# SwiGLU over 8192 rows: the one-row first tile moved to the end

## The chip, the cores and the metric

The kernel runs on one core of one Trainium2 chip, with the other cores idle. The metric is the device time of one execution in microseconds. One execution of the kernel was also recorded by the hardware profiler; its page names lines of the kernel (L54 is line 54) and these engines and queues: ACT (the scalar engine, here silu), DVE (the vector engine, here the product), POOL (GpSimd) and SP (the sync engine). All data between device memory (HBM) and on-chip memory (SBUF, 128 partitions) goes through the core's 16 DMA engines. A transfer is issued by SP, ACT or POOL; q1 is SP's queue, q10 is ACT's and q0 is POOL's.

## The reference

```python
# x: (8192, 8192) float32
def reference(x):
    a, b = np.split(x, 2, axis=-1)
    silu_b = b / (1 + np.exp(-b))
    return a * silu_b
```

Each row of x holds 4096 values of `a` and then 4096 of `b`; the result has 4096 values per row. 268.4 MB are read and 134.2 MB written, and there is nothing to reuse.

## The kernel before, in words

The 8192 rows are cut into 33 tiles. `rows[i]` (line 23) says how many consecutive rows each of the 128 partitions gets of tile i: one for the first, two for the next 31, one for the last. A two-row tile takes 256 rows of x: a load of 8.39 MB (64 KB in a piece per partition) and a store of 4.19 MB (32 KB in a piece per partition). A one-row tile is half of that on both sides.

There are three slots in SBUF, each as large as a two-row tile, and tile i uses slot i % 3. In a slot silu overwrites `b` (line 54), the product goes to the front of the same slot (line 56), and the store reads it from there (line 63). So a slot is free for tile i + 3 only when the store of tile i has landed: the load on line 45 waits for `stored[i - 3]`. These are the only waits that matter. `behind` leaves out all others that the tile framework would add, and the order of instructions is the written one (`manual_schedule`).

Before the loop, the loads of tiles 0, 1 and 2 are issued by SP (line 67). Then for each tile the loop does the compute (`swiglu`), issues the store and issues the load three tiles on. The stores of tiles 0 to 29 are issued by ACT, but those of tiles 17 and 19 by POOL. The stores of the last three tiles (30, 31 and 32) are issued by SP, whose program order is: load 31, load 32 (which waits for store 29), store 30, store 31, store 32. Each waits in turn, so none of them passes the one ahead.

The compute of a tile is one ACTIVATE and one TENSOR_TENSOR over the whole tile, with two exceptions, where both are cut into two pairs: tile 0 (one row) by column halves, and the second to last tile (two rows) by rows.

Of the kernel before, what the change touches and what calls it, by code (L numbers as in the profile page):

```python
# [1 line left out]

# [4 lines left out]

_SILU = mybir.ActivationFunctionType.Silu


@with_exitstack
def kernel(
    ctx: ExitStack,
    tc: tile.TileContext,
    x: bass.AP,
    out: bass.AP,
):
    nc = tc.nc
    N, M = x.shape  # L20
    half = M // 2
    P = nc.NUM_PARTITIONS
    rows = [1] + [2] * (N // (2 * P) - 1) + [1]
    first = [P * sum(rows[:i]) for i in range(len(rows))]
    last = len(rows) - 1

    pool = ctx.enter_context(tc.tile_pool(name="sbuf", bufs=1))
    ctx.enter_context(tc.manual_schedule())
    slots = [pool.tile([P, 2 * M], x.dtype, name=f"slot{s}") for s in range(3)]
    touched = [[] for _ in slots]  # L30
    newest = {}
    landed, made, stored = {}, {}, {}

    def behind(inst, s, *targets):
        for t in touched[s]:
            if t not in targets and t is not newest.get(inst.ins.engine):
                tc.declare_no_dep(inst.ins, t.ins, reason="ordered by the other waits")
        touched[s].append(inst)
        newest[inst.ins.engine] = inst
        return inst  # L40

    def load(i):
        s, r = i % 3, rows[i]
        src = x[first[i] : first[i] + P * r].rearrange("(p r) m -> p (r m)", r=r)
        inst = nc.sync.dma_start(out=slots[s][:, : r * M], in_=src)  # L45
        behind(inst, s, *([stored[i - 3]] if i >= 3 else []))
        landed[i] = inst

    def swiglu(i, k0, k1, c0, c1):
        s, r = i % 3, rows[i]  # L50
        v = slots[s][:, : r * M].rearrange("p (k s c) -> p k s c", k=r, s=2)
        to = slots[s][:, : r * half].rearrange("p (k c) -> p k c", k=r)
        b = v[:, k0:k1, 1, c0:c1]
        gate = nc.scalar.activation(out=b, in_=b, func=_SILU)  # L54
        behind(gate, s, landed[i])
        prod = nc.vector.tensor_mul(out=to[:, k0:k1, c0:c1], in0=v[:, k0:k1, 0, c0:c1], in1=b)  # L56
        behind(prod, s, gate, *([made[i]] if i in made else []))
        made[i] = prod

    def store(i, engine):  # L60
        s, r = i % 3, rows[i]
        dst = out[first[i] : first[i] + P * r].rearrange("(p r) m -> p (r m)", r=r)
        inst = engine.dma_start(out=dst, in_=slots[s][:, : r * half])  # L63
        behind(inst, s, made[i])
        stored[i] = inst

    for i in range(3):
        load(i)
    for i in range(last + 1):
        if i == 0:  # L70
            swiglu(i, 0, 1, 0, half // 2)
            swiglu(i, 0, 1, half // 2, half)
        elif i == last - 1:
            swiglu(i, 0, 1, 0, half)
            swiglu(i, 1, 2, 0, half)
        else:
            swiglu(i, 0, rows[i], 0, half)
        if i < last - 2:
            store(i, nc.gpsimd if i in (17, 19) else nc.scalar)
            load(i + 3)  # L80
        else:
            store(i, nc.sync)


# [1 line left out]
_INS = ['x']  # L86
_OUTS = [((8192, 4096), 'float32')]


# [23 lines left out]
```

## Time and profile before

| | |
|---|---|
| median of 3 runs | 935.07 us (934.93 to 935.09) |
| the profiled execution | 935.77 us, span 934.0 us |
| DVE busy | 278.5 us, 35 instructions |
| ACT busy | 226.6 us, 36 instructions (one is a table load of 1.3 us) |
| DMA | 402.67 MB, 431 GB/s over the span |
| two-row store on ACT's queue | 27 of them, 36.3 us from issue to landing (median) |
| two-row store on POOL's queue | 2 of them, 33.0 us |
| load on SP's queue | 34.9 us (median of 31) |
| one ACTIVATE of 128x8192, 128x4096, 128x2048 | 7.03, 3.61, 1.90 us |
| one TENSOR_TENSOR of 128x8192, 128x4096, 128x2048 | 8.69, 4.42, 2.29 us |

The span is what the profiler saw of the execution; the time around it belongs to the launch. "Busy" counts an engine's own instructions; the DMA row on the page gives the mean busy share of the 16 DMA engines in 40 equal slices of the span (9 is 90% or more). In a windows view, each line is a stretch of the span with its length, the busy times of DVE, ACT and POOL with instruction counts, the clock of the matrix engine (not used here), the DMA share and the GB/s. A packet is counted where it ends, so a short window can read above or below what was moving. In a timeline, each line has start, time, engine and line, operation, operand shapes and count, and in brackets how long the engine had been idle and what ended that; an issue that stands for several (x4) has the time from the first to the last. The chain view follows the work that ended last back from the end, each step with its start and its time.

### The profile page before, as it was taken

To read this page: it belongs to the slowest core of one execution; us is meant where nothing else is said; L and a number is where in the kernel's file an instruction comes from. 1 tells how busy PE (TensorE), PEld (TensorE's weight loads), DVE (VectorE), ACT (ScalarE), POOL (GpSimd) and SP (SyncE) were. 2 spreads that over 40 slices of the span, in tenths; PEclk is the share of its full clock that TensorE was granted. 3 is DMA by queue.
4 is the path that set the end of the run, shared out by engine and by line. 5 is a ranking of instruction groups with operands and counts; after the bars stand their busy time and mean duration, and the time that the engine had idled before them with its cause. 6 is when DMAs were issued, how large, how long until landed. Compare 5 with 4: busy or idle time off the path is not lost.

```text
span 934.0 us, 215 instructions
## 1 busy us (share of the span) xinstructions
DVE 278.5 (30%) x35; ACT 226.6 (24%) x36; POOL 1.4 (0%) x6
## 2 busy tenths in 40 slices
DVE  1131333123331233311333113332133321333242
ACT  2332023320333203332023320333202333023330
POOL 0000000000000000000000000000000000000000
DMA  9999999999999999999999999999999999999998
GB/s 404 404 466 410 427 449 427 448 422 453 406 455 420 428 446 449 425 418 457 408 445 431 425 439 436 448 427 429 446 406 449 428 427 448 428 425 462 435 406 383
DMA packets 9505, 402.67 MB, mean 431 GB/s; under 512 B 1056, under 2 KB 1056, under 8 KB 1056
## 3 DMA queue, kind: packets, MB, share of 16 engines
q1 hardware_dynamic: 5184, 278.92, 69.1%
q10 hardware_dynamic: 4032, 115.35, 28.6%
q0 software_dynamic: 288, 8.39, 2.1%
q14 instruction: 1, 0.01, 0.0%
HBM read 268.44 MB, written 134.22 MB: 431 GB/s over the span
## 4 chain that ended last, share of the span: by engine, by line
DMA 78%; DVE 11%; ACT 9%; another core or an unknown queue 1%; issue 0%; SPq 0%; ACTq 0%
DMA slot<-in_x_dram 40%; DMA out_dram<-slot 37%; DVE slot L56 11%; ACT slot L54 9%; SPq L45 0%; ACTq L63 0%
## 5 line engine op out<-in xcount | busy, mean ns | idle before, releaser
L56 DVE TENSOR_TENSOR slot<-slot 128x8192 f32<-128x8192 f32 (+2 forms) x35 | 278.5, 7960 | 638.5 <-ACT slot L54 638.4
L54 ACT ACTIVATE slot<-slot 128x8192 f32<-128x8192 f32 (+2 forms) x35 | 225.3, 6443 | 685.2 <-DMA slot<-in_x_dram 685.2
L63 POOL DMA_DIRECT2D out_dram<-slot x2 | 1.2, 598 | 569.8 <-DVE slot L56 569.8
L54 ACT ACT_TABLE_LOAD x1 | 1.3, 1283 | 0.7 <-PEq L97 0.7
L97 POOL MEMSET const-bfloat16-1.0<- 128x1 bf16 x1 | 0.1, 101 | 0.0
L97 POOL MEMSET const-float32-0.0<- 128x1 f32 x1 | 0.1, 98 | 0.2 <-issue 0.2
L97 POOL MEMSET const-float32-1.0<- 128x1 f32 x1 | 0.1, 98 | 0.0
L97 POOL MEMSET const-uint8-127<- 128x1 uint8 x1 | 0.1, 98 | 0.0
## 6 DMA issues: line engine op xcount, KB each, us to landing
out_dram<-slot ACTq DMA_DIRECT2D x27, 4096.0 KB, 36.3
slot<-in_x_dram SPq DMA_DIRECT2D x2, 4096.0 KB, 13.7
out_dram<-slot POOLq DMA_DIRECT2D x2, 4096.0 KB, 33.0
out_dram<-slot SPq DMA_DIRECT2D x2, 4096.0 KB, 20.5
out_dram<-slot ACTq DMA_DIRECT2D x1, 2048.0 KB, 28.1
out_dram<-slot SPq DMA_DIRECT2D x1, 2048.0 KB, 16.1
slot<-in_x_dram SPq DMA_DIRECT2D x31, 34.9
```

Of the source, the lines that this page charges most:

```text
L54: gate = nc.scalar.activation(out=b, in_=b, func=_SILU)
L56: prod = nc.vector.tensor_mul(out=to[:, k0:k1, c0:c1], in0=v[:, k0:k1, 0, c0:c1], in1=b)
L63: inst = engine.dma_start(out=dst, in_=slots[s][:, : r * half])
L97: nc = _bacc.Bacc("TRN2", target_bir_lowering=False, num_devices=1)
```

## The change

The list of rows per partition becomes 31 twos and then two ones. Tile 0 is now a two-row tile, cut by rows into two pairs of instructions, as the second to last tile was. The second to last tile is now a one-row tile and has one pair, as the last. The number of tiles, the number of loads and stores of each size, the slots, the three loads ahead and the engines that issue are unchanged; tiles 1 to 30 have the same sizes as before and begin 128 rows earlier in x, and the tile of each index keeps its slot and its issuing engine.

```diff
-    rows = [1] + [2] * (N // (2 * P) - 1) + [1]
+    rows = [2] * (N // (2 * P) - 1) + [1, 1]
     first = [P * sum(rows[:i]) for i in range(len(rows))]
     last = len(rows) - 1
...
     for i in range(last + 1):
         if i == 0:
-            swiglu(i, 0, 1, 0, half // 2)
-            swiglu(i, 0, 1, half // 2, half)
-        elif i == last - 1:
             swiglu(i, 0, 1, 0, half)
             swiglu(i, 1, 2, 0, half)
         else:
```

## The prediction

> **What bounds the kernel now.** I read the page's head and its queue table first, then windows over the whole run and over its ends, then the timeline, the chain and the DMA issues.
>
> ```profile
> span 934.0 us, 215 instructions
> DVE 278.5 (30%) x35; ACT 226.6 (24%) x36; POOL 1.4 (0%) x6
> DMA  9999999999999999999999999999999999999998
> ...
> q1 hardware_dynamic: 5184, 278.92, 69.1%
> q10 hardware_dynamic: 4032, 115.35, 28.6%
> q0 software_dynamic: 288, 8.39, 2.1%
> ```
>
> The two compute engines are busy under a third of the span. The three queues' packets took 69.1 + 28.6 + 2.1 = 99.8% of 16 engines' span, 932.1 of 934.0 us. So the 16 DMA engines are the bound, and only about 1.9 us of the span is not their packet time.
>
> ```profile
> 0.00:1.00 1.00, 0.00 (x0) 0.27 (x1) 0.20 (x4) 1.00 0.00 0
> ...
> 583.87:873.88 290.01, 86.92 (x10) 70.29 (x11) 0.00 (x0) 1.00 1.00 434
> ...
> 932.00:933.00 1.00, 0.00 (x0) 0.00 (x0) 0.00 (x0) 1.00 0.04 16
> 933.00:934.00 1.00, 0.00 (x0) 0.00 (x0) 0.00 (x0) 1.00 0.00 0
> ```
>
> The last two columns are DMA share and GB/s. The engines stand still in the first microsecond and in the last two, and work at a share of 1.00 and 434 GB/s in between. A two-row tile moves 8.39 MB in and 4.19 MB out; at 434 GB/s that is 19.3 + 9.7 = 29.0 us, which is the distance of the tiles in the timeline (583.87, 612.88, 641.88).
>
> ```profile
> 0.74 47.06 SPq L45 DMA_DIRECT2D slot<-in_x_dram  x4
> 12.88 3.71 ACT L54 ACTIVATE slot<-slot 128x2048 f32<-128x2048 f32 x2 [10.86 <-DMA slot<-in_x_dram]
> 14.82 4.49 DVE L56 TENSOR_TENSOR slot<-slot 128x2048 f32<-128x2048 f32 x2 [14.82 <-ACT slot L54]
> 19.35 0.38 ACTq L63 DMA_DIRECT2D out_dram<-slot  x1
> ...
> 864.66 29.33 SPq L45 DMA_DIRECT2D slot<-in_x_dram  x2
> 873.88 7.03 ACT L54 ACTIVATE slot<-slot 128x8192 f32<-128x8192 f32 x1 [21.97 <-DMA slot<-in_x_dram]
> 880.94 8.69 DVE L56 TENSOR_TENSOR slot<-slot 128x8192 f32<-128x8192 f32 x1 [20.31 <-ACT slot L54]
> 894.04 23.32 SPq L63 DMA_DIRECT2D out_dram<-slot  x3
> 899.22 7.12 ACT L54 ACTIVATE slot<-slot 128x4096 f32<-128x4096 f32 x2 [18.31 <-DMA slot<-in_x_dram]
> 902.87 8.96 DVE L56 TENSOR_TENSOR slot<-slot 128x4096 f32<-128x4096 f32 x2 [13.23 <-ACT slot L54]
> 908.93 3.62 ACT L54 ACTIVATE slot<-slot 128x4096 f32<-128x4096 f32 x1 [2.59 <-DMA slot<-in_x_dram]
> 912.58 4.42 DVE L56 TENSOR_TENSOR slot<-slot 128x4096 f32<-128x4096 f32 x1 [0.75 <-ACT slot L54]
> ```
>
> The idle times in brackets are compute waiting for loads. The last load is issued at 893.66 and lands by 908.9; the last product ends at 917.0, and stores alone run until 932.
>
> ```profile
> 860.67 32.98 DMA out_dram<-slot
> ...
> 893.66 15.24 DMA slot<-in_x_dram
> ...
> out_dram<-slot ACTq DMA_DIRECT2D x1, 2048.0 KB, 28.1
> ```
>
> The chain goes through the slots (store, then the load that waited for it). It names whose transfer was in the way; it is not a sum of delays, because the DMA engines are full meanwhile. The last line, the only one-row store on ACT's queue, serves below.
>
> **The DMA work.** Before: 31 two-row and two one-row loads, as many stores. After: the same counts and sizes. On q1 there are 36 transfers either way (33 loads, three stores), on q10 28 and on q0 two. 5184 packets over 36 transfers is 144 each, of which the page counts 16 as under 512 B (1056 over 66 transfers), so each of 128 partition lines is one packet: 64 KB for a two-row load, 32 KB for a two-row store or one-row load, 16 KB for a one-row store. At 434/16 = 27.1 GB/s per engine these take 2.42, 1.21 and 0.60 us, and an engine has 8 of each transfer. Packet work removed: 0; added: 0. q10 gains 2.1 MB that q1 loses. The change can therefore pay only by idle time, of which 1.9 us exists, and can cost only by opening new idle time.
>
> **Compute.** The two 128x2048 pairs of tile 0 go (ACT 3.7, DVE 4.5 us). The 30 whole pairs stay; of 128x4096 there are four pairs instead of three: two on the new tile 0 and one on each one-row tile. Before: 30 x 8.692 + 3 x 4.425 + 2 x 2.288 = 278.6 us on DVE; after: 30 x 8.692 + 4 x 4.425 = 278.5. One instruction less on each engine. All of it lies beside transfers: cost 0.
>
> **The start.** The first transfer needs about 2.4 us beyond its bytes: issued at 0.74, landed at 12.86, and 4.19 MB at 434 GB/s are 9.7. The first load of 8.39 MB then lands at 0.74 + 2.4 + 19.3 = 22.5. Its two halves take what the two halves of the two-row tile at 899.22 took until 911.83, 12.6 us, so the first store is issued at 35.1 instead of 19.35. All three first loads, 25.2 MB, are issued in the first microseconds and would keep the engines full alone until 0.74 + 2.4 + 58.0 = 61.1. The 15.8 us of later start are hidden by these loads with 26 us to spare; without that cover they would cost 15.8. Load 3 waits for store 0 at SP, with nothing ahead of its turn but loads. Taken: 0.
>
> **The middle.** A slot's round is 3 x 29.0 = 87 us: 15.75 of compute, a load and a store. At first store plus load landing are 36.3 + 34.9 us, after the two POOL stores 33.0 + 38.5 (806.69 to 844.86 is 38.2). Only their split moves. After the change, store 0 competes with two-row loads at 2.42 + 1.21 us a pair of packets: 29 us, landing near 35.1 + 1.0 + 29 + 1.4 = 66.5 (of the 2.4 us I put 1.0 before the bytes and 1.4 after). At 36.1 the loads still have some 10.3 MB, which at two thirds of 434 GB/s last until 71.8, so load 3, issued at 66.5, waits behind load 2 and lands at 71.8 + 29 + 1.4 = 102.2. Store 1 lands at 65.1 + 29 + 1.4 = 95.5 and issues load 4, so each queue always has its next transfer, with a few us to spare. At DMA share 1.00, a later load is an earlier store and costs nothing. ACT's queue is passed by one more two-row store instead of a one-row one; POOL's stores stay at indices 17 and 19, now 4.19 MB later in the rows. Taken: 0.
>
> **The tail.** Let T be the landing of load 30, now the last two-row one. Store 28 has landed at T - 9.2 (864.66 against 873.86), which issues load 31, one row; it starts when load 30's data end, about T - 1.4. Until then store 29 got one 32 KB packet per 64 KB packet; with some 9.5 us at 3.63 a pair, 2.6 of its 8 packets. The other 5.4 go one for one against load 31's 32 KB packets, 13.1 us, to T + 11.7. Load 31 then has 2.6 left, alone, 3.1 us, to T + 14.8. Load 32 needs 1.4 us for store 29's landing and 1.0 for its own first bytes: it arrives at T + 14.1. That cover of 0.7 us is thin. With the earlier split (34.9) the same steps give 1.6 packets, 2.0 us of cover against 2.4, a hole of 0.4 us. What lies under it is the full latency, 2.4 us, if load 31 is through before store 29. Nothing excludes small gains at transfer edges, at most some 0.5 us of the 1.9 idle. I take 0, since the split of the late rows is the nearest, and keep -0.5 and +2.4.
>
> Behind it the queue is full: store 30 is made at T + 15.75 and stands behind load 32 on q1, load 32's data end at T + 24.5, stores 30 and 31 last until T + 39, and store 32 is ready by T + 24.5 + 1.4 + 8.1 (908.93 to 917.0) + 1.0 = T + 35. SP now holds store 30 from 889.6, when it is made, until 894.04, behind load 32's wait; after the change load 32 is issued by T + 13.1 and store 30 is made later, so nothing is held.
>
> The row behind the split is the one-row store on ACT's queue: 8 x (2.42 + 0.60) + 2.4 = 26.6 us if packets alternate; equal bytes would give 12.1, two load bytes per store byte 16.9. Measured: 28.1. So packets alternate. In the Trainium skill, the page DMA: Bandwidth & Descriptors, section Queues, rings and completion order, says the same of each engine: it goes round its queues and takes a whole packet from one before it switches; by that rule load 31 and store 29 share evenly and the sum is 0, while two load bytes per store byte (what 8.39 and 4.19 MB in 29 us each look like) would end load 31 at T + 13.6 and store 29 at T + 15.3, and the hole would be the full 2.4. The trace agrees with the page in this row.
>
> **Sum:** 0 + 0 + 0 + 0 on the profiled execution's 935.77 us (934.0 of span and 1.77 around it), which stands 0.70 above the median of 935.07; so 935.8 profiled and 935.1 in the median.
>
> **The rivals.** *A hole in the tail* (slower): load 31 runs out before load 32 arrives. For it: 0.7 us of cover by the sum above, and SP's order, by which store 30 cannot step in. Against it: the alternation. Price 0.4 to 2.4 us, likeliest 1.9, 937.0; it decides when load 31's data end before store 29 lands.
>
> *An exposed start* (slower): the first store's 15.8 us delay reaches the end, 935.1 + 15.8 = 950.9. It would need the loads to be done before 35.1 us; they last until 61.1. The Trainium skill's page Perfetto Trace Analysis, section DMA Optimizations, says that splitting transfers can let work start sooner and finish sooner when DMA engines are generally idle; merging the small first load is the reverse. The trace does not meet its condition: 99.8% busy.
>
> *A gain*: four tile distances are longer than 29.0 us (30.25 and 30.21, 29.44 and 29.45), 3.4 us together, and another phase avoids them: 931.7. Against it: the windows over them move 434 to 441 GB/s, so what the loads lost the stores had.
>
> *Holes in every round* (slower): both queues empty at once for 0.1 us a tile, 31 x 0.1, 938.2. Against it: each has its next transfer waiting.
>
> **How the numbers follow.** No change 0.70 (935.1, own range 934.6 to 935.9); hole in the tail 0.20; exposed start 0.04; gain 0.03; holes in every round 0.03. About 0.2%, 1.87 us, is what a measurement of this kernel can tell from no change: below 933.2 is faster, above 936.9 slower. Half the tail-hole case lies above: slower 0.10 + 0.04 + 0.03 = 0.17, faster 0.03, same 0.80. The range goes from 934.5 to 937.5 (935.1 + 2.4) and leaves out 0.10.
>
> **What the profile after would show.** The first store issue near 35 us on ACT's queue and load 3 near 66; tile distances of 29.0; queue shares that again sum to 932 us; load 31 and load 32 landing 10 us apart, with no 1 us window near zero between; last product some 10 us before the end. I am wrong if a window near load 32's issue falls to nothing, if queue shares sum well below 99.8% of the span, or if the packets themselves take longer (the sum rises with the span).

## The result and the profile after

The changed kernel takes 938.09 us in the median of 22 runs (936.69 to 938.94) against 935.07 us for 22 runs of the kernel before (934.89 to 939.29): a ratio of 1.0027, 95% interval 1.0020 to 1.0033. The median is 3.0 us slower, just beyond the 0.2% that the prediction named as its bound, and 0.6 us above the top of its range. The profiled execution took 937.95 us, 2.18 us more than the one of before, which stood 0.70 above its median; its span is 936.2.

The head of the page after and its queue table (packets, MB, share of 16 engines' span):

```profile
span 936.2 us, 213 instructions
DVE 278.5 (30%) x34; ACT 226.5 (24%) x35; POOL 1.4 (0%) x6
...
q1 hardware_dynamic: 5184, 276.83, 68.6%
q10 hardware_dynamic: 4032, 117.44, 29.1%
q0 software_dynamic: 288, 8.39, 2.1%
```

The counts of packets are those of before, and the three shares again sum to 99.8%. But they are shares of a longer span: the times of all packets, summed and divided by 16 engines, are 933.9 us, against 931.9 before. The DMA engines are as full as ever by this table; the same packets took 1.9 us longer. In the tail some 32 KB packets took up to 2.46 us where 1.21 is the median, so lost time is counted there as packet time, and the table cannot show a hole of this size. What shows it is the distance between two landings. The timeline of the changed kernel, first its start and then its tail:

```profile
0.73 127.46 SPq L45 DMA_DIRECT2D slot<-in_x_dram  x6
22.63 7.12 ACT L54 ACTIVATE slot<-slot 128x4096 f32<-128x4096 f32 x2 [20.62 <-DMA slot<-in_x_dram]
...
35.27 0.38 ACTq L63 DMA_DIRECT2D out_dram<-slot  x1
46.59 7.03 ACT L54 ACTIVATE slot<-slot 128x8192 f32<-128x8192 f32 x1 [16.84 <-DMA slot<-in_x_dram]
```

```profile
888.82 7.03 ACT L54 ACTIVATE slot<-slot 128x8192 f32<-128x8192 f32 x1 [22.00 <-DMA slot<-in_x_dram]
895.88 8.69 DVE L56 TENSOR_TENSOR slot<-slot 128x8192 f32<-128x8192 f32 x1 [20.33 <-ACT slot L54]
901.32 0.33 SPq L45 DMA_DIRECT2D slot<-in_x_dram  x1
904.53 3.62 ACT L54 ACTIVATE slot<-slot 128x4096 f32<-128x4096 f32 x1 [8.68 <-DMA slot<-in_x_dram]
...
915.89 3.62 ACT L54 ACTIVATE slot<-slot 128x4096 f32<-128x4096 f32 x1 [7.75 <-DMA slot<-in_x_dram]
```

The chain shows what load 32 waited for, store 29:

```profile
875.58 25.73 DMA out_dram<-slot
901.30 0.02 issue
901.32 14.55 DMA slot<-in_x_dram
```

Load 32 is issued at 901.32, when store 29 has landed; load 31 has landed by 904.53 and load 32 by 915.89. The two landings are 11.36 us apart, where the 4.19 MB need 9.7; in the kernel before they were 9.71 apart (899.22 and 908.93). That is 1.65 us of DMA time lost between two loads. The windows between these landings, before and then after (the last two columns are DMA share and GB/s), say the same:

```profile
899.22:908.93 9.71, 5.96 (x2) 7.12 (x3) 0.00 (x0) 1.00 1.00 432
```

```profile
904.53:915.89 11.36, 4.47 (x2) 3.61 (x1) 0.00 (x0) 1.00 0.97 378
```

The rate falls from 432 to 378 GB/s while the share of busy time is still 0.97.

### The profile page after: what moved, and what is told of

Read it like the earlier page. It is cut to its first block, busy times and chain, and to the rows that moved or that the text cites. A ratio compares the mean times of both kernels' runs of the same rounds, so it can differ in the third digit from the quotient of the medians.

```text
span 936.2 us, 213 instructions
## 1 busy us (share of the span) xinstructions
DVE 278.5 (30%) x34; ACT 226.5 (24%) x35; POOL 1.4 (0%) x6
## 4 chain that ended last, share of the span: by engine, by line
DMA 78%; DVE 11%; ACT 9%; another core or an unknown queue 1%; issue 0%; SPq 0%; ACTq 0%
DMA slot<-in_x_dram 41%; DMA out_dram<-slot 36%; DVE slot L56 11%; ACT slot L54 9%; SPq L45 0%; ACTq L63 0%
## 5 line engine op out<-in xcount | busy, mean ns | idle before, releaser
L56 DVE TENSOR_TENSOR slot<-slot 128x8192 f32<-128x8192 f32 (+1 forms) x34 | 278.5, 8190 | 645.5 <-ACT slot L54 645.4
L54 ACT ACTIVATE slot<-slot 128x8192 f32<-128x8192 f32 (+1 forms) x34 | 225.2, 6627 | 692.3 <-DMA slot<-in_x_dram 692.3
```

## The experiments

The cover of a waiting load is the load data still queued when it is issued; where the cover is too short, a hole opens. Two theories stood against each other. *Tail*: load 32, which waits for store 29, comes when load 31 is nearly through, and the queues run dry. *Start*: something in the new first tile costs, although the DMA engines have loads queued until 61 us.

**The wait taken away.** Tile 32 uses the free second half of tile 31's slot, so that its load needs only store 28.

```diff
+    def place(i):
+        if i == last:
+            return (last - 1) % 3, rows[i], M
+        return i % 3, rows[i], 0
...
-        behind(inst, s, *([stored[i - 3]] if i >= 3 else []))
+        behind(inst, s, *([stored[min(i, last - 1) - 3]] if i >= 3 else []))
...
-            load(i + 3)
+            if i + 3 < last:
+                load(i + 3)
+            if i + 3 == last - 1:
+                load(last)
```

> The changed kernel, but the load of tile 32 goes to the unused second half of slot 1, beside tile 31, and is issued right behind load 31: it no longer waits for store 29. If the hole in the tail (load 32 arriving after load 31's data have run out, about 1.5 us by the distance of their landings, 11.4 us against 9.7 before) is the main cost, loads 31 and 32 land 9.7 us apart or less and the time falls by about 1.5 us, to 936.6. If the cost lies at the start, the time stays at 938.1.

Measured: 936.33 us (935.97 to 937.09), ratio to the kernel before 1.0011 (1.0002 to 1.0019). In its timeline the landings are 9.72 us apart:

```profile
850.26 29.79 SPq L50 DMA_DIRECT2D slot<-in_x_dram  x3
...
904.22 3.62 ACT L59 ACTIVATE slot<-slot 128x4096 f32<-128x4096 f32 x1 [8.66 <-DMA slot<-in_x_dram]
...
913.94 3.62 ACT L59 ACTIVATE slot<-slot 128x4096 f32<-128x4096 f32 x1 [6.11 <-DMA slot<-in_x_dram]
```

The last load has now been issued by 850.26 + 29.79 = 880.1, far ahead. The tail theory gave 936.6; 1.8 us are gone. But 1.2 us over the kernel before (935.15 in this group of runs) remain, and the tail does not hold them.

**The start undone.** Tile 0 is loaded and stored as two one-row parts, the first computed by column halves as before; `part`, `swiglu_part` and `store_part` load, compute and store one such part.

```diff
-    for i in range(3):
-        load(i)
...
+    part(0, 0)
+    part(0, 1)
+    load(1)
+    load(2)
...
-            swiglu(i, 0, 1, 0, half)
-            swiglu(i, 1, 2, 0, half)
+            swiglu_part(0, 0, 0, half // 2)
+            swiglu_part(0, 0, half // 2, half)
+            store_part(0, 0)
+            swiglu_part(0, 1, 0, half)
+            store_part(0, 1)
```

> The changed kernel, but tile 0 is loaded and stored in two one-row parts, the first computed by column halves, so the first store is one row and goes out near 19.4 us as in the kernel before. If the start costs about 0.5 us, the time falls to about 937.6; if only the tail costs, it stays at 938.1 (one load and one store more).

Measured: 937.28 us (935.20 to 938.54), ratio 1.0016 (1.0007 to 1.0026): 0.8 us less than the changed kernel. The profiled execution is the fastest of its eleven, 935.20 us, and in it the landings of loads 31 and 32 are 9.70 us apart, though load 32 still waits for store 29:

```profile
847.72 52.29 SPq L45 DMA_DIRECT2D slot<-in_x_dram  x3
...
903.32 3.62 ACT L55 ACTIVATE slot<-slot 128x4096 f32<-128x4096 f32 x1 [8.69 <-DMA slot<-in_x_dram]
...
913.02 3.62 ACT L55 ACTIVATE slot<-slot 128x4096 f32<-128x4096 f32 x1 [6.08 <-DMA slot<-in_x_dram]
```

This time there is no hole: half of the engines had landed load 31 3.3 us after load 32's issue, where it was 1.9 in the changed kernel's trace. The cover is thus not the same in every trace; more of it below.

**Both edits.**

> Both edits, the early load 32 and the split first tile. If hole and start together are the whole difference, 935.1 to 935.6, the time of the kernel before; if something else in between costs, it stays above 936.5.

Measured: 935.24 us (935.04 to 936.97), ratio 1.0002 (0.9991 to 1.0013), the median of the kernel before. Within the interval, about 1 us either way, tail and start together are the whole difference, and nothing in the tiles between them was seen to cost. The median needs care: the eleven times fall into two groups, six at 935.0 to 935.2 and five at 936.5 to 937.0. The profiled execution is of the second group (936.52); its landings at the end are in step (9.69 us apart), its packets take 932.1 us an engine, 0.2 more than in the kernel before, and its last landing comes 1.47 us after that of the fifteenth of the sixteen engines. That points to one engine behind the others, not to a hole.

**The tail alone.** The kernel before keeps its start, but its last rows are cut 2, 1, 1, 1; the last two tiles share a slot and are issued together, behind the wait for store 29.

```diff
-    rows = [1] + [2] * (N // (2 * P) - 1) + [1]
+    rows = [1] + [2] * (N // (2 * P) - 2) + [1, 1, 1]
...
```

> The kernel before with its start unchanged, but its last five rows per partition cut as 2, 1, 1, 1 (the last two share a slot and are issued together), so that load 31 is a one-row load and load 32 waits for store 29 as in the changed kernel. If the tail hole is the main cost, about 935.1 + 1.5 = 936.6; if the start is, 935.1.

Measured: 937.99 us (935.99 to 938.77), ratio 1.0023 (1.0014 to 1.0031): more than expected. Its three last landings:

```profile
889.12 3.62 ACT L59 ACTIVATE slot<-slot 128x4096 f32<-128x4096 f32 x1 [8.68 <-DMA slot<-in_x_dram]
...
899.50 3.62 ACT L59 ACTIVATE slot<-slot 128x4096 f32<-128x4096 f32 x1 [6.77 <-DMA slot<-in_x_dram]
...
911.03 3.62 ACT L59 ACTIVATE slot<-slot 128x4096 f32<-128x4096 f32 x1 [7.91 <-DMA slot<-in_x_dram]
```

They are 10.38 and 11.53 us apart, 2.5 us over two times 9.7. The second distance is odd, since those two loads were issued together. This version also has one tile more, which is a rival for its time.

**The same cut, but covered.** Loads 31 and 32 now share a slot and are issued together after store 28; the load that waits for store 29 is load 33, with both in front of it. The edit is against the version just shown.

```diff
     def place(i):
+        if i == last - 1:
+            return (last - 2) % 3, rows[i], M
         if i == last:
-            return (last - 1) % 3, rows[i], M
+            return (last - 1) % 3, rows[i], 0
...
-        behind(inst, s, *([stored[min(i, last - 1) - 3]] if i >= 3 else []))
+        behind(inst, s, *([stored[i - 3 - (i >= last - 1)]] if i >= 3 else []))
...
```

> The kernel with the old start and last rows 2, 1, 1, 1, but now the load that waits for store 29 is the last one, behind two one-row loads that were issued together, so 9.7 us more of load are queued when it is issued. If the thin cover of that wait made the 2.8 us of the version before this one, 935.1 to 935.4; if the extra tile or the one-row shapes did, it stays near 938.

Measured: 935.32 us (935.20 to 937.20), ratio 1.0002 (0.9993 to 1.0011), with the landings in step again:

```profile
888.75 3.62 ACT L61 ACTIVATE slot<-slot 128x4096 f32<-128x4096 f32 x1 [8.68 <-DMA slot<-in_x_dram]
...
898.48 3.62 ACT L61 ACTIVATE slot<-slot 128x4096 f32<-128x4096 f32 x1 [6.12 <-DMA slot<-in_x_dram]
...
908.19 3.62 ACT L61 ACTIVATE slot<-slot 128x4096 f32<-128x4096 f32 x1 [6.09 <-DMA slot<-in_x_dram]
```

The shapes, the counts and the wait on store 29 are those of the version before; what differs is which load waits, and so what stands in the queue ahead of it. So neither the extra tile nor one-row shapes cost anything that shows, and the difference between the two versions, 2.7 us by the medians and 2.0 by the ratios, is the thin cover.

**One load instead of two, and the changed kernel beside it.** The last two rows are loaded as one two-row tile (32 tiles of two rows), computed and stored by rows. In the same group of runs the changed kernel was timed once more.

```diff
-    rows = [2] * (N // (2 * P) - 1) + [1, 1]
+    rows = [2] * (N // (2 * P))
```

> The changed kernel, but the last two one-row tiles are loaded as one two-row tile (32 tiles, all of two rows), computed and stored by rows in two parts. No load waits behind a one-row load any more. If the thin cover makes the tail hole, 936.3 like the version with the early load 32; if two one-row stores and computations at the end cost, 938.1.

> The changed kernel itself, beside the others of this call: 938.1, if it differs from the version with one two-row load at the end only by the tail hole, 1.8 us above that version.

Measured: 936.11 us (935.38 to 936.28), ratio 1.0008 (0.9999 to 1.0017), and 937.72 us (937.62 to 938.95, five runs) for the changed kernel, ratio 1.0033 (1.0020 to 1.0045). In the second trace of the changed kernel the hole is there again, 11.30 us between the landings:

```profile
904.27 3.62 ACT L54 ACTIVATE slot<-slot 128x4096 f32<-128x4096 f32 x1 [8.66 <-DMA slot<-in_x_dram]
...
915.57 3.62 ACT L54 ACTIVATE slot<-slot 128x4096 f32<-128x4096 f32 x1 [7.68 <-DMA slot<-in_x_dram]
```

The hole is worth 1.6 us here, and avoiding it in this way gives about the same time as the early load 32 (936.33).

**What at the start costs.** Four versions with the early load 32 vary only the start. In one, tile 0 is computed whole, which delays the first store:

```diff
-        if i == 0:
-            swiglu(i, 0, 1, 0, half)
-            swiglu(i, 1, 2, 0, half)
-        else:
-            swiglu(i, 0, rows[i], 0, half)
+        swiglu(i, 0, rows[i], 0, half)
```

> The early load 32 (no tail hole), with tile 0 computed in one piece, so that the first store goes out 3.1 us later, at 38.4 us, after the load packets that begin at 36 to 38.5 us. If the start's 1.2 us come from the first store entering just at the boundary between loads 1 and 2 (load packets of 3.7 us instead of 2.4 near 38.7), another moment changes them: 935.2 to 935.8. If they come from the first store being two rows, or from loads of 64 KB packets alone, the time stays at 936.3.

Measured: 936.85 us (936.23 to 937.39), ratio 1.0018 (1.0009 to 1.0027). The first store went out at 38.55, and the time did not fall:

```profile
38.55 0.38 ACTq L68 DMA_DIRECT2D out_dram<-slot  x1
...
72.18 7.03 ACT L59 ACTIVATE slot<-slot 128x8192 f32<-128x8192 f32 x1 [23.06 <-DMA slot<-in_x_dram]
```

But the edit did more than move the store. Load 2 has landed by 72.18, and store 0, now later, lands only at 72.34; load 3 waits for it and is issued at 72.36 with no load ahead of it, a wait as in the tail with no cover at all. Packets that begin at 75.4 to 78.9 take 1.34 us an engine too long in this trace, while those near the first store's entry, at 41.1 to 41.7, take 0.96, against 1.18 with the early load 32 alone (how this is worked out stands below). So this run does not settle whether the moment of the first store matters. In two others only the stores or only the load of tile 0 are split into rows:

```diff
+            swiglu_part(0, 0, 0, half)
+            store_part(0, 0)
+            swiglu_part(0, 1, 0, half)
+            store_part(0, 1)
```

> The early load 32, with tile 0 loaded in one piece but stored in two one-row stores, the first near 30.7 us. If the size or the moment of the first store makes the start's cost, the time falls to 935.2 to 935.6; if the size of the first load does, it stays at 936.3.

```diff
+    parts = [part(0, 0), part(0, 1)]
+    load(1)
+    load(2)
```

> The early load 32, with tile 0 loaded in two one-row parts but stored in one two-row store, near 30.5 us. If the first load's size makes the start's cost, the time falls to 935.2 to 935.6; if the store's size does, it stays at 936.3; if the moment does, it moves to anywhere between.

Measured: 935.85 us (935.36 to 936.90), ratio 1.0009 (1.0001 to 1.0018), with two stores, between the two values expected; 936.50 us (935.32 to 938.23), ratio 1.0011 (1.0002 to 1.0020), with two loads. In one table, all with the early load 32, medians and ratios to the kernel before:

| tile 0 | one two-row store | two one-row stores |
|---|---|---|
| one two-row load | 936.33, 1.0011 | 935.85, 1.0009 |
| two one-row loads | 936.50, 1.0011 | 935.24, 1.0002 |

Only the cell with both splits, which also lets the first store out at 19 us, stands at the time of the kernel before. By the ratios neither split does much alone, and the intervals of all four cells overlap, so which part of the start costs is not settled.

The packet records of the traces point to the same place. I took each packet's time less the median of its size, summed and divided by 16 engines. In the changed kernel, load packets that begin at 36 to 41 us, after the first store was issued at 35.27, take 1.27 us an engine too long (most of them 3.3 to 3.9 instead of 2.42 us each). With the early load it is 1.18. In the kernel before, two smaller groups, at 21.8 (0.21) and 31.2 (0.55, the last packets of load 1), give 0.77. With two one-row stores it is 1.0. So in each of these traces load packets are slow soon after the first store is issued, and with a two-row store some 0.4 us more than in the kernel before. The version with the tail alone, whose start is that of the kernel before, has 1.0, so such sums differ by 0.2 us from trace to trace. The 0.4 us are less than half of the 1.2 us; the rest stays open (the traced execution with the early load, 935.97, was itself 0.4 us below its median).

**A still smaller first store.** The kernel before, with the first one-row store cut into two column halves:

```diff
-            swiglu(i, 0, 1, 0, half // 2)
-            swiglu(i, 0, 1, half // 2, half)
+            for c in (0, half // 2):
+                swiglu(i, 0, 1, c, c + half // 2)
+                dst = out[: P, c : c + half // 2]
+                inst = nc.scalar.dma_start(out=dst, in_=slots[0][:, c : c + half // 2])
+                stored.setdefault(i, []).append(behind(inst, 0, made[i]))
```

> The kernel before, with the one-row store of tile 0 cut by column halves into two stores, the first near 17 us with packets of half the size. If the stall at the entry of the first store grows with the size of its packets (so far about 1.0 us an engine with 32 KB packets at once, 0.2 to 0.5 with 16 KB), it shrinks further and the time is 934.6 to 935.0; if it is the second stall, at the end of load 1 (0.5 us), that counts, 935.0 to 935.2, no change.

Measured: 935.25 us (935.10 to 936.25), ratio 1.0004 (0.9995 to 1.0012). No gain, and there are two groups of slow packets again (0.19 us an engine near 30.5 and 0.56 near 52.4). No version of these beats the kernel before.

## Why the prediction was wrong

**The floor.** "The change can therefore pay only by idle time" held: packets and bytes came out as counted, and DVE was busy for 278.5 us, as worked out. That the change could cost only by new idle time held too, except that such time hides inside packets. The prediction named both signs, shares that fall and packets that take longer; it was the second.

**The tail, "Taken: 0", was mis-sized.** The mechanism of the rival *A hole in the tail*, given a chance of 0.20, was right, and most of its steps fit. With T = 888.79, load 31 was issued at T - 9.2, as predicted; store 29 landed at T + 12.5 (T + 13.1) and load 31 at T + 15.7 (T + 16.2). The trace's packets alternate one for one between q1 and q10 from 887 to 899 us (78 and 81 packets), as said.

What failed is the step "Load 32 needs 1.4 us for store 29's landing and 1.0 for its own first bytes". The 2.4 us came from the first transfer, which had no other queue beside it. Here store 29's last packets end near 899.2, and on each engine a load packet of 1.21 us goes ahead of the small packet that tells of the store's end; the landings of the 16 engines come from 900.44 to 901.30, 1.2 to 2.1 us after the data. Load 31's data end at 902.5 to 903.3 on most engines (predicted T + 14.8 = 903.6). The first packets of load 32 follow at once but end as if they had begun at 902.9 to 903.7 (predicted T + 14.1 = 902.9). So the cover of 0.7 us, called thin, was none.

That late arrival shows as 0.3 us an engine. Load 32 landed at T + 27.1 instead of T + 25.9, because another 1.1 us an engine lie at its end, and for these the prediction had no step. The runs show that they come with the thin cover and go with it; how they arise stays open. The price, for which 0.4 to 2.4 us with 1.9 as the likeliest had been given, is 1.6 to 1.8 by the early load and the single load, and 2.0 to 2.8 in the version with the tail alone. The choice among the bounds was wrong: a difference of 0.7 us between two sums of latencies is less than these latencies are known to. (The rival's figures for two load bytes per store byte, T + 13.6 and T + 15.3, should have been T + 13.1 and T + 14.8, since the same packets are moved; nothing hangs on it.)

**The start, "Taken: 0", missed a cost.** The later first store is indeed hidden by loads: it went out at 35.27 (predicted 35.1) and nothing like 15.8 us appears, so that rival is out. But 1.1 to 1.2 us by the medians (0.8 to 1.0 by the ratios) stay when the tail is mended, and the prediction had no term for it: what a store costs the loads beside it when it enters was taken as its packets alone. The slow load packets near that entry show about 0.4 us of it; where the rest comes from is not shown.

**The middle, 0, held.** Tile distances are 29.0 us, and the version with both ends mended is at the time of the kernel before, within 1 us. Load 3's predicted issue at 66.5 came at 69.8, without harm.

With 1.6 to 1.8 us for the tail and 1.1 to 1.2 for the start the 3.0 us are accounted for, but these terms are steps between the same medians and so must add up. Measured from the other side, the tail alone costs 2.8 us and undoing the start alone gives back 0.8, so each term is known to about 1 us. The top of the range, 937.5, held the tail's bound alone; two small costs together went over it.

## What to carry to other kernels

In a kernel that keeps its DMA engines full, every load that waits for a store must have enough bytes queued ahead of it to outlast that store's landing, the issue and the new load's first bytes. In this kernel's traces 1.9 to 2.1 us from the issue of the waiting load to the landing of the load ahead did not suffice; 3.3 us, 1.4 MB at 434 GB/s, did. A smaller transfer just ahead of such a wait takes this cover away; check it at every change of tile size, and give the small tile a free half slot or put the larger load in front. The share of busy time does not show a hole of 1 to 2 us; compare the distances of landings with bytes over rate.

## What the runs showed of the hardware that I had not expected

**The threshold.** From the issue of the load that waits until half of the engines had landed the load ahead of it there were 1.9 us in the changed kernel's trace (901.3 to 903.2), 2.1 in its second one and in the version with the tail alone, and a hole in each; 3.3 us in the trace with the start undone (899.7 to 903.0), and none. Where between 2.1 and 3.3 us the threshold lies was not tried.

**A hole shows in two places.** Of the changed kernel's extra packet time in the tail, 0.32 us an engine lies in packets that begin near 902.7, where load 32 enters, and 1.1 us in packets that begin at 910 to 913, at the end of that load (0.19 and 1.27 in its second trace). Both are gone in the versions with cover. In the version with the tail alone the late part (1.0 us, at 905 to 908) falls into the load after the one that waited, which is its odd second distance. In all three traces it falls on the last packets of the last load, just before the stores that follow on SP's queue begin. Why most of the loss is recorded there stays open.

**One DMA engine can fall behind and stay there.** In the changed kernel's trace 15 of 16 engines have landed load 1 by 44.50, the last at 46.57, and that last one is what the ACTIVATE at 46.59 waits for. For each two-row load after it the last engine lands 1.2 to 2.1 us after the fifteenth. In the kernel before the same begins at tile 5: fifteen engines by 145.38, the last at 146.75. So the longest of the tile distances that the rival *A gain* took for phase, 30.25, is one engine getting behind; the fifteenth engine's distance there is 29.03. The 29.45 is again the last engine's (28.60 for the median engine). In those of 30.21 and 29.44 the engines come later together (30.21 and 29.43 for the median engine).

At the end of the profiled execution before, the last engine is 0.75 us behind the fifteenth, and that execution took 0.70 us more than the median; with both edits it is 1.47 behind, and the execution took 1.3 us more than the median. In the other traces it is 0.65 or less. This goes far to explain the two groups of times, but it is not the 3 us: in the second trace of the changed kernel the last landing is never more than 0.7 us behind the fifteenth, and it took 937.66.
